# The FFN of a hybrid diffusion step: chunks of three and six token blocks, the six in scaled fp16 pairs

## The chip, the cores and the metric

The kernel runs on one core of a Trainium2 chip. The metric is the device time of one execution in microseconds (us). The engines are called as in the profile: PE (TensorE, matmuls), PEld (its weight loads), DVE (VectorE), ACT (ScalarE), POOL (GpSimd) and SP (SyncE, which issues most DMAs). A chance of "faster" or "slower" means by more than 0.3%.

## What is computed

One layer over 128 context tokens and 1024 latent tokens, D_MODEL = 1024. Attention and an mLSTM read one input projection and share one output projection; then comes a SwiGLU FFN with D_FF = 2816. All tokens use the same weights. The part that the change touches:

```python
def swiglu(h, w_gu, w_down):
    g, u = jnp.split(h @ w_gu, 2, axis=-1)
    return (jax.nn.silu(g) * u) @ w_down

# in trunk_layer, behind attention and mLSTM
    mix = jnp.concatenate([attn_o, hm], axis=-1) @ w_out
    x = x + g1 * mix
    h2 = rmsnorm(x, norm2_w) * (1 + sc2) + sh2
    x = x + g2 * swiglu(h2, w_gu, w_down)
# the result is rmsnorm(x, final_norm_w)
```

Inputs and results are fp32. `w_gu` is 1024 x 5632 (gate, then up), `w_down` is 2816 x 1024.

## The kernel before

The 1152 tokens are nine blocks of 128 (block 0 is the context). Three blocks make a chunk, so there are three chunks: c = 0, 1, 2. A precise product is made of three matmuls: both operands are split into a high and a low half, and high x high, high x low and low x high are added up in PSUM. In the input projection the halves are scaled fp16 (`Scaled`, `linear_tok`, `head_project`). In the output projection and the FFN they are fp32r (a 4-byte type that PE reads in one pass).

**FFN.** D_FF is 22 tiles of 128 columns. `gate_up` makes, for each tile and a whole chunk (384 tokens), gate and up: `products` runs 8 x 3 matmuls of 384 columns for each (L1271 to L1273). The tanh form of silu times up gives `tn` (L1298 to L1300), split into `hl`. `down` takes a group of four or five tiles (`GROUPS`, `LAST`) and adds their product with `w_down` to the residual `x1` (`three_blocks`, matmuls of 512 columns, L1090 to L1092; `add_gated`, L1079 and L1080). Every piece of weights is loaded and split for every chunk anew by `load_piece`: a DMA of 512 KB on SP's queue into `raw` (two buffers), ACT's copy to the high half (L152), the subtraction for the low half, two in three on POOL and one on DVE (L135 through `sub`). So `w_gu` and `w_down` are read three times.

**Around it.** `prefill` adds the mLSTM half of the output projection to `x1` of all blocks; blocks 6 to 8 go through x1_d in DRAM by way of the three `t2` buffers, which the loads of `hm` use too. `attention(c)` works head by head: score matmuls (L1000) into the only score buffer `S`, a maximum on DVE (L1002), exp on ACT (L1003), an fp16 pair of the probabilities (L1006, L1007), transposes by DMA, and for two heads together the values (L1024, L1025). `attn_out` adds the attention half of the output projection, `norm2` makes the FFN's input. `finish` and `down_last` make the final norm and write out.

**Order.** `weave(main, side, n_main, n_side)` runs a main generator and takes steps of a side one at a fixed rate. Chunk 0's FFN has attention of chunk 1 woven in (17 of 22 tiles), chunk 1's FFN that of chunk 2, chunk 2's FFN stands alone. The first part of attention of chunk 1 runs before, beside `prefill` and `attn_out(0)`. A planner (`schedule_with_timeline_sim`) then orders each engine's instructions by the program's order, by `hot` priorities and by its own model of time. After that each engine's queue runs in order, and so does SP's queue of DMAs. PSUM has four banks for `mm`, one for `po` and three for `S`.

The loop around the chunks, and the last one's end:

```python
            weave(main, chain(previous(c, cur), att), 18 * sum(nf for _, nf in GROUPS[:NG]) - 24, 50)
            emit(att)
            emit(attn_out(c + 1, nxt, oT, out_gates()))
            emit(groups(c, cur, GROUPS[NG:-1]))
            ...
            weave(chain(down(c, cur, f0, nf, 0), down(c, cur, f0, nf, 1)), n2, 6 * nf, 8)
```

## Time and profile before

| | us |
|---|---|
| runs (three) | 1620.82, 1625.18, 1626.45 |
| median | 1625.18 |
| span of the profiled execution (no other time of it is given) | 1626.0 |
| PE clock, mean share granted | 0.972 |
| attention of chunk 0 and prefill | about 460 to 640 |
| FFN of chunk 0 with attention of chunk 1 | about 640 to 1000 |
| FFN of chunk 1 with attention of chunk 2 | about 1000 to 1300 |
| FFN of chunk 2 | about 1300 to 1613 |

A row of busy time by stage gives the stretch, its length, then busy us and number of instructions of each engine, the granted share of PE's clock, the DMA engines' mean busy share and their GB/s. A row of single instructions in order of time gives start, length, engine, line, operation, output and inputs; one "x6" at its end stands for six in a row. A row of a group gives busy time, mean ns of one, and the engine's idle time ahead with what ended it. The bar of a matmul is its whole way through the array, so bars overlap: the distance of starts is the pace. Some matmul records can be missing.

### The profile page before, as it was taken

Reading aid. Unit: us, or ns where it says so; the run is one execution under the profiler, and the core shown is the slowest. Engines: PE = TensorE matmul, PEld = TensorE weight load, DVE = VectorE, ACT = ScalarE, POOL = GpSimd, SP = SyncE. Lnnn points to the kernel's source line nnn. Section 1 sums busy time; section 2 is a strip of 40 time slices with the busy share of each in tenths; the row PEclk is TensorE's granted clock in tenths of the full one; section 3 lists DMA queues with packets and bytes.
Section 4 is the critical chain, followed back from the end, with each engine's and each line's share of the span. In section 5 each row is a group of like instructions: output and inputs, shape, how many; then the busy total and the mean of one; then the engine's idle time right before and its main releaser. Section 6 shows DMA issues by size and latency. Waiting matters only on the chain. (4 is left out here: it accounts for less than half of the span.)

```text
span 1626.0 us, 23528 instructions
## 1 busy us (share of the span) xinstructions
PE 1517.4 (93%) x8688; PEld 1258.8 (77%) x8688; DVE 970.8 (60%) x2059; ACT 732.5 (45%) x1251; POOL 606.5 (37%) x387
## 2 busy tenths in 40 slices
PE   5899899899879768999999999999999999999996
PEld 2745566575557557998989899898898989899995
DVE  3843364958987665467672646777674474432445
ACT  3744252434544554545643344565562453333332
POOL 0411020404344514443435354444344444545443
PEclk8999999999999878999999999999999999999998
DMA  9355352201156855767873546777684445545441
GB/s 357 94 165 130 101 147 58 84 21 46 41 198 147 195 107 112 168 168 174 187 184 112 149 141 219 187 184 173 156 183 128 134 142 170 152 126 149 130 142 66
DMA packets 386313, 232.73 MB, mean 143 GB/s; under 512 B 169910, under 2 KB 346502, under 8 KB 386198
## 3 DMA queue, kind: packets, MB, share of 16 engines
q1 hardware_dynamic: 384342, 228.04, 52.7%
q10 hardware_dynamic: 1856, 3.19, 0.6%
q8 instruction: 68, 1.11, 0.3%
q14 instruction: 47, 0.39, 0.1%
HBM read 181.16 MB, written 11.69 MB: 119 GB/s over the span
## 5 line engine op out<-in xcount | busy, mean ns | idle before, releaser
L135 POOL TENSOR_TENSOR wlo<-raw,whi 128x1024 fp32r<-128x1024 f32 x146 | 357.8, 2454 | 445.7 <-ACT whi L152 407.9
L152 ACT CAST whi<-raw 128x1024 fp32r<-128x1024 f32 x219 | 224.4, 1025 | 375.9 <-DMA raw<-in_w_gu_dram 137.8
L1272 PE MATMUL mm<-aTl,whi 128*128 128x384 f32 (+2 forms) x1088 | 364.7, 335 | 0.7 <-POOL aTl L135 0.7
L1273 PE MATMUL mm<-aTh,wlo 128*128 128x384 f32 (+2 forms) x1088 | 364.4, 335 | 0.0
L1271 PE MATMUL mm<-aTh,whi 128*128 128x384 f32 (+2 forms) x1088 | 363.4, 336 | 0.7 <-DVE tn L1299 0.7
L1272 PEld LDWEIGHTS mm<-aTl,whi 128*128 128x128 f32 x1088 | 205.9, 189 | 1.7 <-POOL aTl L135 0.9
L1271 PEld LDWEIGHTS mm<-aTh,whi 128*128 128x128 f32 x1088 | 205.4, 189 | 2.0 <-DVE tn L1299 1.3
L1273 PEld LDWEIGHTS mm<-aTh,wlo 128*128 128x128 f32 x1088 | 205.8, 189 | 0.1
L135 DVE TENSOR_TENSOR wlo<-raw,whi 128x1024 fp32r<-128x1024 f32 (+1 forms) x73 | 88.1, 1206 | 142.2 <-ACT whi L152 141.7
L1090 PE MATMUL mm<-whi,hl 128*128 128x512 f32 x372 | 145.8, 397 | 1.5 <-ACT hl L1303 1.4
L1091 PE MATMUL mm<-wlo,hl 128*128 128x512 f32 x372 | 146.9, 397 | 0.0
L1092 PE MATMUL mm<-whi,hl 128*128 128x512 f32 x372 | 144.3, 396 | 0.7 <-POOL hl L135 0.7
L1007 DVE SCALAR_TENSOR_TENSOR pl<-pr,st,ph 128x1152 f16<-128x1152 f32 (+1 forms) x72 | 107.8, 1498 | 39.4 <-ACT ph L1006 39.4
L488 PE MATMUL wi<-ipair,hT 128*128 128x384 f16 (+2 forms) x392 | 128.2, 327 | 2.8 <-ACT ipair L216 2.8
L489 PE MATMUL wi<-ipair,hT 128*128 128x384 f16 (+2 forms) x392 | 128.1, 327 | 0.0
L490 PE MATMUL wi<-ipair,hT 128*128 128x384 f16 (+2 forms) x392 | 127.1, 326 | 0.0
L135 POOL TENSOR_TENSOR hl<-tn,hl 128x384 fp32r<-128x384 f32 x66 | 84.2, 1276 | 105.0 <-ACT hl L1303 105.0
L1003 ACT ACTIVATE pr<-S,st 128x1152 f32<-128x1152 f32 (+1 forms) x72 | 81.1, 1127 | 89.1 <-DVE st L1002 86.1
L1299 DVE SCALAR_TENSOR_TENSOR tn<-tn,mm 128x384 f32<-128x384 f32 (+2 forms) x68 | 36.7, 540 | 137.9 <-PE mm L1273 97.5
L1080 DVE TENSOR_TENSOR x<-x,t 128x512 f32<-128x512 f32 x102 | 116.5, 1163 | 0.8
L1000 PE MATMUL S<-kst,qT 128*128 128x384 f32 (+1 forms) x400 | 88.3, 355 | 19.6 <-ACT pr L1003 19.2
L1002 DVE TENSOR_REDUCE st<-S 128x1 f32<-128x1152 f32 (+1 forms) x72 | 88.9, 1234 | 18.3 <-PE S L1000 17.8
(353 smaller groups left out, 2684.6 us busy)
## 6 DMA issues: line engine op xcount, KB each, us to landing
raw<-in_w_gu_dram SPq DMA_DIRECT2D x132, 512.0 KB
raw<-in_w_down_dram SPq DMA_DIRECT2D x60, 512.0 KB
a<-in_w_ada_dram SPq DMA_DIRECT2D x32, 512.0 KB
gl<-g_d SPq DMA_DIRECT2D x36, 256.0 KB
aw<-in_w_ada_dram SPq DMA_DIRECT2D x16, 512.0 KB
iraw<-in_w_in_dram SPq DMA_DIRECT2D x32, 256.0 KB
raw<-in_w_out_dram SPq DMA_DIRECT2D x15, 512.0 KB
x<-in_x_sample_dram SPq DMA_DIRECT2D x13, 512.0 KB
```

What stands on the lines that cost most here:

```text
L135: (dve if eng == "dve" else pool).tensor_tensor(out=out, in0=full, in1=hi, op=ALU.subtract)
L152: nc.scalar.copy(hi[:, :n], raw[:, :n])
L488: mm(ps[:, :n], ah, wh[:, k % 2, c0 : c0 + n], start=(k == 0), stop=False)
L489: mm(ps[:, :n], ah, wl[:, k % 2, c0 : c0 + n], start=False, stop=False)
L490: mm(ps[:, :n], al, wh[:, k % 2, c0 : c0 + n], start=False, stop=(k == KD - 1))
L1080: eng.tensor_tensor(out=x1[:, cs], in0=x1[:, cs], in1=t, op=ALU.add)
L1090: mm(ps, ah, wh[:, k % 2, :], start=(k == 0), stop=False)
L1091: mm(ps, ah, wl[:, k % 2, :], start=False, stop=False)
L1092: mm(ps, al, wh[:, k % 2, :], start=False, stop=(k == nk - 1))
L1271: mm(ps, wh[:, k, :], th[:, k, :], start=(k == 0), stop=False)
L1272: mm(ps, wh[:, k, :], tl[:, k, :], start=False, stop=False)
L1273: mm(ps, wl[:, k, :], th[:, k, :], start=False, stop=(k == KD - 1))
```

## The change

Chunk 0 keeps its FFN in fp32r. Chunks 1 and 2 run theirs together, six blocks on one reading of the weights, in scaled fp16 pairs.

- Both attentions now run beside chunk 0's FFN: the rest of chunk 1's beside groups 0 and 1, chunk 2's beside groups 2 and 3 together with `norm2(1)`; `norm2(2)` beside the gates of group 4.
- `bound_h2` derives a power of two from the bounds of scale and shift; `norm2` of c > 0 uses scaled copies and writes fp16 pairs.
- `Piece` loads a tile's gate and up (1 MB), measures the sum of squares on ACT, sums it over partitions with a matmul of ones, makes a power of two in eight DVE operations, and converts (ACT the high, DVE the low half): loaded three tiles ahead, measured two ahead, converted one ahead. The first is done within the last `down` of chunk 0.
- `split_down` loads `w_down` tile by tile (512 KB), scales and splits it by partition, and writes the fp16 pair to DRAM (`wd_d`); `down6` reads these four times in quarters, two for each half of the blocks.
- `gate_up6` keeps `tn` of a whole group in fp32; `rescale` finds the group's scale and writes `hl`. Groups are of 10, 8 and 4 tiles (`SIX`). PSUM becomes eight banks.
- `prefill` sends blocks 3 to 8 through x1_d. `down`'s adds for chunk 0 go to POOL.

The diff, cut:

```diff
-LAST = [(0, 5), (5, 5), (10, 4), (14, 4), (18, 4)]
+SIX = [(0, 10), (10, 8), (18, 4)]
+SLOTS = 30
...
+    wd_d = [drp.tile([P, 2, 2, 2, 512], F16, name=f"wd_d{j}") for j in range(NF // 2)]
...
+    def bound_h2():
+        m = gp.tile([P, 4], F32, name="hb2")
+        dve.tensor_reduce(out=m[:, 0:1], in_=scale2, axis=AX.XY, op=ALU.max, apply_absolute_value=True)
+        dve.tensor_reduce(out=m[:, 1:2], in_=shift2, axis=AX.XY, op=ALU.max, apply_absolute_value=True)
...
+        yield from power_scale(gp, one1, m[:, 2:3], h2s)
...
-                    if c < 2:
-                        add_gated(x1s[c][i], ps, g, n, pool)
+                    if c == 0:
+                        add_gated(x1[i], ps, g, n, pool)
                     else:
                         xt = t2()
                         dma(xt, xrow(b)[:, cs])
                         t = t2()
                         dve.tensor_tensor(out=t, in0=ps, in1=g, op=ALU.mult)
                         pool.tensor_tensor(out=xt, in0=xt, in1=t, op=ALU.add)
-                        dma(x1_d[i][:, cs], xt)
+                        dma(x1_d[b - CB][:, cs], xt)
...
+    def split_down():
+        def load(f):
+            t = hp.tile([P, 3, 1024], F32, name=nm("wdt"), tag=f"b{2 + f % 2}")
+            dma(t[:, 0], w_down[f * P : (f + 1) * P, :])
+            return t
+        ahead = [load(0)]
+        for f in range(NF):
+            t = ahead.pop(0)
+            if f + 1 < NF:
+                ahead.append(load(f + 1))
+            yield
+            raw, v = t[:, 0], wds[:, f, :]
+            act(t[:, 2].bitcast(BF16)[:, 0:1024], raw, AF.Abs, accum_out=v[:, 0:1])
+            powers(v, P)
+            yield
...
+            act(o[:, :, 0], raw, AF.Copy, scale=v[:, 2:3])
+            dve.scalar_tensor_tensor(out=o[:, :, 1], in0=raw, scalar=v[:, 2:3], in1=o[:, :, 0], op0=ALU.mult, op1=ALU.subtract)
+            dma(wd_d[f // 2][:, :, f % 2], o)
+            yield
...
+        def measure(self):
+            v = self.v = fp.tile([P, 8], F32, name=nm("fv"), tag="fv", bufs=5)
+            for j, raw in enumerate(self.raw):
+                jk = ft.tile([P, D], BF16, name=nm("jk"), tag="t2", bufs=3)
+                act(jk, raw, AF.Square, accum_out=v[:, j : j + 1])
+        def scales(self):
+            v = self.v
+            ps = bank()
+            mm(ps[:, 0:2], ones, v[:, 0:2], start=True, stop=True)
...
+        def convert(self):
...
+                act(t[:, 0], raw, AF.Copy, scale=sc)
+                dve.scalar_tensor_tensor(out=t[:, 1], in0=raw, scalar=sc, in1=t[:, 0], op0=ALU.mult, op1=ALU.subtract)
...
+    weave(main, att, 18 * 8 - 24, 42)
+    emit(att)
+    one = {"x1": new_x1(1, "b6")}
+    emit(attn_out(1, one, oT, out_gates()))
...
+    weave(groups(0, cur, GROUPS[2:4]), chain(*[norm2(1, one, i) for i in range(CB)], att), 18 * 9, 48)
+    emit(att)
+    two = {"x1": new_x1(2, "b0")}
+    emit(attn_out(2, two, oT, out_gates()))
...
+    weave(gate_up(cur, f0, nf), n2, 12 * nf, 7)
+    emit(n2)
+    first = Piece(0, lambda: wp.tile([P, 1024], F32, name=nm("braw"), tag="raw", bufs=2))
+    emit(down(0, cur, f0, nf, 0))
+    for i, _ in enumerate(down(0, cur, f0, nf, 1)):
+        if i == 0:
+            first.load()
+        elif i == 1:
+            first.measure()
+        elif i == 3:
+            first.scales()
+        elif i == 4:
+            first.convert()
...
+    one["x1"] = new_x1(1, "b1")
...
+    pieces[1].load()
+    pieces[1].measure()
+    pieces[2].load()
...
+    emit(finish(0, cur))
...
+    wd_steps = split_down()
+    for _ in range(4):
+        next(wd_steps)
...
+                    products(ps[:, 0:CT], wh, wl, th, tl)
+                    step = 2 * half + j
+                    if step == 0:
+                        if f + 1 < NF:
...
+                            pieces[f + 1].convert()
+                        if f + 3 < NF:
+                            pieces[f + 3].load()
+                        p.fold()
+                        next(wd_steps, None)
+                    elif step == 1 and f + 2 < NF:
+                        pieces[f + 2].measure()
...
+                    elif step == 3:
+                        if f + 2 < NF:
+                            pieces[f + 2].scales()
+                        next(wd_steps, None)
...
+                act(tn, pg[:, 0:CT], AF.Tanh, scale=p.v[:, 6:7])
+                dve.scalar_tensor_tensor(out=tn, in0=tn, scalar=1.0, in1=pu[:, 0:CT], op0=ALU.add, op1=ALU.mult)
+                dve.scalar_tensor_tensor(out=tn, in0=tn, scalar=p.v[:, 7:8], in1=pg[:, 0:CT], op0=ALU.mult, op1=ALU.mult)
+                jk = ft.tile([P, D], BF16, name=nm("jk"), tag="t2", bufs=3)
+                act(jk[:, 0:CT], tn, AF.Abs, accum_out=g["st"][:, 2 * i + half : 2 * i + half + 1])
...
+        for tn in g["a"]:
+            hl = bp.tile([P, 2, CT], F16, name=nm("hl"), tag="hl", bufs=SLOTS)
+            act(hl[:, 0], tn, AF.Copy, scale=m[:, 1:2])
+            dve.scalar_tensor_tensor(out=hl[:, 1], in0=tn, scalar=m[:, 1:2], in1=hl[:, 0], op0=ALU.mult, op1=ALU.subtract)
...
+    def down6(g):
+        for half in range(2):
+            for n in range(2):
+                banks = [bank() for _ in range(CB)]
+                for j in range(0, g["nf"], 2):
+                    w = down_piece(g, j, n)
+                    for i, ps in enumerate(banks):
+                        b = half * CB + i
+                        down_products(ps, g, j, b, w)
+                        if j + 2 == g["nf"]:
+                            add_gated(x6[b], ps, g6[n], n, inv=g["inv"])
+                        yield
```

`groups6` runs a group's `down6` inside the next group's gates, and the last group's down runs block by block with the final norm, as `down_last` did.

More of the change, by code (lines that the diff above doesn't have):

```diff
@@ L908, in hybrid_step @@
     cc, ss = tables(kw)
-    kwork = k_work(qp, cc, ss, kw)
+    kwork = chain(k_work(qp, cc, ss, kw), bound_h2())
     scan = head_mlstm(2, sts[2])
-    weave(head_project(3, sts[3]), beside((scan, 1.15), (kwork, 0.5)), 56, 56)
+    weave(head_project(3, sts[3]), beside((scan, 1.15), (kwork, 0.55)), 56, 56)
     emit(scan)
@@ L1421, in previous @@
             yield
[L1423 to L1451 removed]
+            o = t[:, 1].bitcast(F16).rearrange("p (n h x) -> p n h x", n=2, h=2)
@@ new lines, in hybrid_step @@
+    main = groups(0, cur, GROUPS[:2])
+    for _ in range(4):
+        next(main)
+    weave(main, att, 18 * 8 - 24, 42)
+    emit(att)
+    one = {"x1": new_x1(1, "b6")}
+    emit(attn_out(1, one, oT, out_gates()))
+    oT = []
+    att = attention(2, oT, set())
+    weave(groups(0, cur, GROUPS[2:4]), chain(*[norm2(1, one, i) for i in range(CB)], att), 18 * 9, 48)
+    emit(att)
+    two = {"x1": new_x1(2, "b0")}
+    emit(attn_out(2, two, oT, out_gates()))
+    f0, nf = GROUPS[-1]
+    n2 = chain(*[norm2(2, two, i) for i in range(CB)])
@@ new lines, in hybrid_step @@
+    bp = ctx.enter_context(tc.tile_pool(name="bp", bufs=1, reuse_waits="tile"))
+    psum["mm"] = ctx.enter_context(tc.tile_pool(name="p8", bufs=8, space=PSUM, reuse_waits="tile"))
+    pieces = [first] + [Piece(f) for f in range(1, NF)]
+    pieces[1].load()
+    pieces[1].measure()
+    pieces[2].load()
+    h6 = [(t["h2"][:, 0], t["h2"][:, 1]) for t in (one, two)]
+    x6 = one["x1"] + two["x1"]
+    emit(finish(0, cur))
+    g6 = []
+    for n in range(2):
+        gl = ft.tile([P, 512], F32, name=nm("gl"), tag=("gl", "gx")[n], bufs=1)
+        dma(gl, g_d[1, 1:2, n * 512 : (n + 1) * 512].to_broadcast([P, 512]))
+        g6.append(gl)
@@ new lines, in groups6 @@
+    def groups6(grps):
+        held = None
+        for g in grps:
+            ups = gate_up6(g)
+            if held is not None:
+                r = rescale(held)
+                for _ in range(2):
+                    yield next(ups)
+                next(r)
+                for _ in range(2):
+                    yield next(ups)
+                emit(r)
+                for _ in range(2):
+                    yield next(ups)
+                if g["nf"] > 4:
+                    yield from down6(held)
+                    yield from ups
+                else:
+                    yield from ups
+                    d = down6(held)
+                    for _ in range(6):
+                        yield next(d)
+                    r = rescale(g)
+                    next(r)
+                    for _ in range(6):
+                        yield next(d)
+                    emit(r)
+                    yield from d
+            else:
+                yield from ups
+            held = g
```

255 lines of the change are left out of this document (153 added, 102 removed).

## The prediction

> **What bounds the kernel now.** I read the page's engine totals first, then busy time by stage, then single matmuls in order of time.
>
> ```profile
> span 1626.0 us, 23528 instructions
> PE 1517.4 (93%) x8688; PEld 1258.8 (77%) x8688; DVE 970.8 (60%) x2059; ACT 732.5 (45%) x1251; POOL 606.5 (37%) x387
> ...
> 460.00:640.00 180.00, 141.79 (x731) 114.43 (x731) 122.97 (x233) 90.72 (x137) 70.03 (x41) 0.89 0.64 150
> 640.00:1000.00 360.00, 355.50 (x1991) 326.38 (x1990) 217.36 (x327) 173.51 (x232) 152.51 (x73) 0.99 0.63 158
> 1000.00:1240.00 240.00, 236.09 (x1345) 215.69 (x1344) 156.20 (x215) 128.99 (x169) 99.75 (x47) 1.00 0.73 180
> 1240.00:1600.00 360.00, 358.17 (x1879) 331.77 (x1878) 165.95 (x229) 126.88 (x167) 172.80 (x86) 1.00 0.47 141
> 1600.00:1626.00 26.00, 13.20 (x57) 10.36 (x55) 16.99 (x54) 6.39 (x15) 3.85 (x3) 0.80 0.17 61
> ```
>
> The rows by stage give, behind the length, the busy us of PE, weight loads, DVE, ACT and POOL, then granted clock, DMA share and GB/s. From 640 us on (the FFN of all three chunks, with attention of chunks 1 and 2 woven in) PE is idle 4.5 + 3.9 + 1.8 = 10.2 us in 960, at a clock of 0.99 to 1.00. So PE sets the time there, and only two things can move it: how fast PE goes through its list, or idle time that is put in. Busy bars of matmuls overlap, so the pace is read from their starts:
>
> ```profile
> 1440.13 0.34 PE L1272 MATMUL mm<-aTl,whi 128*128 128x384 f32 x1
> ...
> 1441.86 0.34 PE L1273 MATMUL mm<-aTh,wlo 128*128 128x384 f32 x1
> 1442.04 0.39 PE L1090 MATMUL mm<-whi,hl 128*128 128x512 f32 x1
> ...
> 1445.99 0.39 PE L1092 MATMUL mm<-whi,hl 128*128 128x512 f32 x1
> 100.59 0.33 PE L488 MATMUL wi<-ipair,hT 128*128 128x384 f16 x1
> ...
> 102.86 0.33 PE L490 MATMUL wi<-ipair,hT 128*128 128x384 f16 x1
> 424.78 0.38 PE L488 MATMUL mm<-ipair,hT 128*128 128x512 f16 x1
> ...
> 425.86 0.38 PE L490 MATMUL mm<-ipair,hT 128*128 128x512 f16 x1
> 1072.01 0.28 PE L1025 MATMUL po<-plT,vs 128*128 128x256 f16 x1
> ...
> 1072.78 0.27 PE L1024 MATMUL po<-phT,vs 128*128 128x256 f16 x1
> ```
>
> Between the first two rows lie 10 steps: 1.73/10 = 0.173 us for 384 columns of fp32r. The next two: 17 steps, 3.95/17 = 0.232 us for 512. In fp16, which the input projection already uses, 14 steps of 2.27 give 0.162 for 384, and 5 steps of 1.08 give 0.216 for 512. Fp32r costs some 7% more per column.
>
> **The change, part by part.** *Pace.* One tile of 128 FFN columns takes, for three token blocks, 2 x 8 x 3 = 48 matmuls of 384 columns (gate, up) and 3 x 2 x 3 = 18 of 512 (down). The number of matmuls stays; for six of nine blocks they become fp16. Gate and up: 22 x 48 x 2 = 2112 x (0.173 - 0.162) = 23.0 us. Down: 22 x 18 x 2 = 792 x (0.2324 - 0.216) = 13.0 us. Together **-36.0 us**, all on PE's path. This is the whole source of gain: the weights are read and split less often, but POOL (37%), ACT and DMA were not in PE's way.
>
> The Trainium skill, page "TensorE: Matmul & The Clock Gate", section "Back-to-back issue gap", speaks against it: its formula for the warm gap is columns / 2.4 + 2.5 ns, whatever the data type, that is 162.5 and 215.8 ns. The fp16 rows agree with it (0.162, 0.216); the fp32r rows (0.173, 0.232) don't. By that formula the type gains nothing, this term is zero and the sum would be 36 us higher.
>
> *Matmuls added.* Each gate/up tile gets one fp32 matmul of two columns with a matrix of ones (`scales`), which sums the squares over partitions. Three groups and the bound of h2 add a transpose and a two-column matmul each.
>
> ```profile
> L324 PEld LDWEIGHTS wi<-strip_sel,part 128*128 128x128 f32 x32 | 3.7, 191 | 3.2 <-ACT part L356 3.2
> L324 PE MATMUL wi<-strip_sel,part 128*128 128x2 f32 x32 | 3.9, 252 | 1.4 <-ACT part L356 1.4
> ```
>
> Nearest is a two-column fp32 matmul: its weight load of 0.19 us hides under the matmul before (0), or lies bare with the matmul behind it (0.44). I take the load alone: 22 x 0.19 = **+4.2** (0 to 9.7). The four others, two small matmuls of 0.25 each with a little between: 4 x 0.55 = **+2.2**. Each `scales` also waits for ACT's measure, and behind it in PE's queue stand the next products; the measure is issued two runs of 24 matmuls, 7.8 us, ahead of it, which covers some 2.5 us of work on ACT.
>
> *Chunk 0 carries both attentions.* So far attention of chunk 1 is woven into 17 tiles of chunk 0 and that of chunk 2 into 17 of chunk 1. Now the rest of the first lies in 8 tiles and the second in 9, beside norm2 of chunk 1.
>
> ```profile
> 640.00:860.00 220.00, 26.40 (x120) 21.57 (x120) 0.98 0.73 169
> 1000.00:1220.00 220.00, 29.74 (x144) 24.99 (x144) 1.00 0.76 186
> ...
> 1060.00:1120.00 60.00, 60.00 (x349) 54.42 (x348) 46.55 (x61) 34.40 (x46) 25.33 (x11) 1.00 0.73 173
> ...
> L1002 DVE TENSOR_REDUCE st<-S 128x1 f32<-128x1152 f32 x64 | 86.6, 1353 | 17.6 <-PE S L1000 17.3
> L1007 DVE SCALAR_TENSOR_TENSOR pl<-pr,st,ph 128x1152 f16<-128x1152 f32 x64 | 103.5, 1617 | 39.2 <-ACT ph L1006 39.2
> L1029 DVE SCALAR_TENSOR_TENSOR oT<-po,vsc,ol 64x128 f32<-64x128 f32 x72 | 24.6, 342 | 16.9 <-ACT ol L1027 15.6
> L1299 DVE SCALAR_TENSOR_TENSOR tn<-tn,mm 128x384 f32<-128x384 f32 x64 | 35.3, 552 | 136.1 <-PE mm L1273 97.5 <-ACT tn L1298 38.0 <-issue 0.3
> L135 DVE TENSOR_TENSOR wlo<-raw,whi 128x1024 fp32r<-128x1024 f32 x67 | 83.9, 1252 | 118.0 <-ACT whi L152 117.6 <-issue 0.4
> L1079 DVE TENSOR_TENSOR t<-mm,gl 128x512 f32<-128x512 f32 x106 | 70.7, 684 | 39.5 <-PE mm L1092 17.6 <-DMA gl<-g_d 10.4 <-PE mm L1358 6.7
> L1245 DVE TENSOR_SCALAR fl<-mm,scale,shift 128x128 f32<-128x128 f32 x66 | 22.5, 403 | 1.8 <-PE mm L114 1.7
> ```
>
> The first two rows count the score matmuls (L1000), six to a head: 24 heads in 220 us, 9.2 us each. In the second new weave 9 tiles take 9 x (48 x 0.173 + 18 x 0.232) = 112 us and 24 heads about 24 x (6 x 0.173 + 9 x 0.11) = 49 (nine matmuls of 256 columns a head): 161/24 = 6.7 us a head. The first weave, 8 tiles and 120/6 = 20 heads, is about as dense: 141/20 = 7.0. DVE per head: 1.35 + 1.62 + 0.34 and about 0.4 of small operations (an estimate) = 3.7. A tile of the FFN: two of 0.55, one lower half in three of its pieces (1.25), six multiplies of 0.68 to four or five tiles (0.9) = 3.3, since the adds now go to POOL; 0.375 tiles a head = 1.2. Norm2 of chunk 1: six halves of 4 x 0.40 and a subtraction of some 0.7 = 14 us, 0.6 a head. That is 5.5 of 6.7, 82%. At 1060 to 1120 DVE was busy 78% and PE 60.00 of 60. So it fits, with little room: I take **+4** (lower bound -5, half the 10.2 of idle time gone; upper bound in the rivals). ACT is lower: its 128.99 of 240 us in the 1000:1240 row, times 9.2/6.7, is 74%.
>
> *Prefill.* Blocks 3 to 5 now go through `t2` buffers and x1_d as 6 to 8 did: six more round trips on SP's queue, each some 512 KB, at a DMA share of 0.64 (row 460:640). All nine hm blocks share the three `t2` buffers, so DVE can wait for a store, and attention's reductions stand behind it. **+1** (0 to 8). `bound_h2` adds some 14 small DVE operations, under 3 us, hidden beside the head projection.
>
> *Entering the six blocks.* The first fp16 tile is loaded, measured, scaled and converted during the last down-projection of chunk 0.
>
> ```profile
> 1352.81 6.72 DMA raw<-in_w_gu_dram
> L199 ACT ACTIVATE jk<-iraw 128x1024 bf16<-128x1024 f32 x20 | 21.2, 1058 | 7.6 <-DMA iraw<-in_w_in_dram 7.3 <-issue 0.3
> L216 ACT ACTIVATE ipair<-iraw,isc 128x1024 f16<-128x1024 f32 x10 | 11.5, 1152 | 1.9 <-PE wi L490 1.8
> L217 DVE SCALAR_TENSOR_TENSOR ipair<-iraw,isc,ipair 128x1024 f16<-128x1024 f32 x10 | 16.0, 1612 | 8.6 <-ACT ipair L216 8.6
> ```
>
> A 512 KB load took 6.7 us to land in the chain of waits; two beside each other I put at 8. Then the second measure (1.06 + 0.19), the sum (0.25), eight DVE operations (1.2), the first high half (1.15): 12 us, with hand-overs 13. Cover: the load stands behind two of 15 units of three matmuls, 13 x 3 x 0.232 = 9 us. Uncovered **+4** (0 to 20). The sum's wait stands in PE's queue ahead of the last down matmuls, and DVE's adds for chunk 0 wait for those.
>
> *Inside the six.* A tile's gate/up lasts 96 x 0.162 = 15.6 us. ACT does two converts (2.3), two measures (2.5), w_down's measure and high half (2.4), two tanh and two absolute sums of 384 columns (an estimate from 1.06 for 1024: about 2.3): 9.5. DVE does two lower halves (3.2), that of w_down (1.6), four multiplies of about 0.55 and some 13 small ones: 9. Both fit, at about 60%. DMA moves 1 MB of w_gu, 0.5 in and 0.5 out of w_down: 2 MB in 15.6 us, 128 GB/s, where 180 was seen. `rescale` has 20 copies each on ACT and DVE, about 12 us, behind 16 us of other products. I take **+2** (0 to 10).
>
> *The end.* A block of the last down now takes PE 24 x 0.216 = 5.2 us; its DVE work is 5.5 to 6.7.
>
> ```profile
> 1612.80 0.40 PE L1358 MATMUL mm<-whi,hl 128*128 128x512 f32 x1
> ...
> 1610.95 1.81 DVE L1080 TENSOR_TENSOR x<-x,t 128x512 f32<-128x512 f32 x1
> ...
> 1616.66 0.68 DVE L1080 TENSOR_TENSOR x<-x,t 128x512 f32<-128x512 f32 x1
> ...
> 1621.35 0.16 DVE L131 SCALAR_TENSOR_TENSOR ry<-rt,ry 128x1 f32<-128x1 f32 x1
> 1621.54 0.75 DVE L1369 SCALAR_TENSOR_TENSOR x<-x,ry,fw 128x512 f32<-128x512 f32 x1
> ```
>
> (Two multiplies of 0.68, as L1079 above, two adds of 0.68 to 1.81, twelve of about 0.16 for the root, one of 0.75.) DVE already starts its last operation 8.7 us after the last matmul. Six blocks instead of three let it fall further behind: **+3** (0 to 6).
>
> *Sum:* -36.0 + 4.2 + 2.2 + 1 + 4 + 4 + 2 + 3 = -15.6, so a span of 1610.4 from 1626.0. The runs' median, 1625.18, is within 1 us of that span, so the forecast is 1610.
>
> **Rivals.**
> 1. *All the new work is hidden.* Only the added matmuls remain: 1626 - 36 + 6.4 = 1596. For it: the old changes of stage cost PE next to nothing (10.2 us in 960). Against: entering the six has an uncovered chain in the program's order.
> 2. *The entry is bound by transfers.* Ahead of the first w_down tile stand in program order 1 MB, 1.5 of x1, 2 more of weights, about 1 of gates and gains: 6 MB, at 180 GB/s 33 us from the first load. If ACT's order puts its measure in front of the second tile's convert, due about 29 us in, that comes at some 36 to 42 us: 7 to 13 us more. Time 1617 to 1630, say 1623: no change that can be measured.
> 3. *Slower: attention binds PE in chunk 0.* In 460:640 PE idled 38.2 us while 130 score matmuls, 21.7 heads, ran (first row): 1.8 us a head, and the score buffer heads the list of waits there (second row):
>
> ```profile
> 460.00:640.00 180.00, 30.67 (x130) 25.00 (x130) 0.89 0.64 150
> ...
> PE S L1000 <- ACT pr L1003: 15.4, 6, 3.7
> ```
>
> If the 24 heads of the second weave ran so, that is 43 us in place of the 4: 1610 - 4 + 43 = 1649; with the first weave at a third of it as well it is beyond 1655, and two thirds as bad in the second alone is 1635. It decides once DVE's 5.5 us and its waits pass 6.7 a head, since one score buffer is shared. Against it stand 78% of DVE with no idle PE.
> 4. *The change doesn't speed PE up:* the 7% belongs to the FFN's stage and not to fp32r, so 1610 + 36 = 1646. The page's formula would have it so. Against: the 256-column fp16 matmuls of attention, in that stage, go at 0.77/7 = 0.110, the fp16 pace (0.162 x 256/384 = 0.108).
>
> **Chances.** About 0.3%, 5 us, is what a measurement can tell from no change: faster is below 1620, slower above 1630. Forecast (1600 to 1620) 0.48; rival 1 0.15; rival 2 with other small losses (1620 to 1630) 0.17; rival 3 0.16; rival 4 0.04. Faster 0.63, same 0.17, slower 0.20. The range 1592 to 1634 takes in all of the forecast and rival 2, most of rival 1 and the mild end of rival 3; about 0.2 is left out. It spans -34 to +8 in the sum, most of the unknown bounds.
>
> **What would show it.** Starts of 384-column matmuls 0.162 apart and of 512-column ones 0.216 in the six's stage; PE idle there below 5 us; a gap of some 4 us before the first six-block tile; in chunk 0, PE idle below 15 us and DVE near 80% in the second weave; DVE's end 10 to 15 us after the last matmul. It is wrong if fp16 goes at 0.173 there, if PE waits on scores or on `scales` by tens of us, or if DVE or ACT come near 90% within the six.

## The result and the profile after

The changed kernel takes 1690.14 us (median of four runs, 1684.76 to 1694.7), the kernel before in the same session 1623.95 (1620.82 to 1626.45): a ratio of 1.0412, 95% interval 1.0381 to 1.0443. It is 66 us slower, where 15 less were forecast. The profiled execution has a span of 1683.0 against 1626.0, so it shows 57 of the 66; the execution profiled after is the fastest of the four.

The head of the page after, to be laid beside the two lines of before:

```profile
span 1683.0 us, 23816 instructions
PE 1514.7 (90%) x8744; PEld 1051.5 (62%) x8744; DVE 983.9 (58%) x2389; ACT 771.3 (46%) x1410; POOL 377.5 (22%) x285
```

PE has as much busy time as before in a longer span. No engine has become full: DVE went from 60% to 58%, ACT from 45% to 46%. So something waits, and the rows by stage (columns as in the prediction's) say where:

```profile
460.00:640.00 180.00, 137.25 (x658) 107.56 (x656) 123.93 (x228) 88.05 (x135) 64.71 (x39) 0.87 0.65 157
640.00:860.00 220.00, 195.71 (x1140) 173.92 (x1139) 141.39 (x223) 117.74 (x159) 93.55 (x48) 0.95 0.66 161
860.00:980.00 120.00, 120.00 (x693) 110.10 (x692) 81.83 (x115) 68.03 (x92) 57.18 (x31) 1.00 0.74 169
980.00:1100.00 120.00, 90.08 (x430) 75.60 (x429) 72.20 (x113) 56.75 (x75) 29.25 (x15) 0.82 0.62 149
1100.00:1160.00 60.00, 51.88 (x261) 41.81 (x260) 30.95 (x82) 33.96 (x51) 20.14 (x13) 0.91 0.68 218
1160.00:1660.00 500.00, 500.00 (x2856) 279.60 (x2854) 231.82 (x562) 195.49 (x358) 3.81 (x3) 1.00 0.38 122
```

The six blocks (1160 to 1660) run PE for 500.00 of 500 us at full clock. All of the loss lies ahead of them: PE is idle 24.3 us in 640 to 860, nothing in 860 to 980, 29.9 in 980 to 1100 and 8.1 in 1100 to 1160, 62 us in a stretch (640 to 1160) where the kernel before had 7.8. The clock granted in the three stages with idle time is 0.82 to 0.95, where before it was 0.98 to 1.00. The list of PE's waits in 640 to 1160 (total, times, longest, us) names no single cause:

```profile
PE S L1023 <- ACT pr L1026: 16.6, 5, 6.7
PE mm L116 <- ACT y L1262: 13.7, 2, 9.3
PE po L1048 <- DMA plT<-pl: 8.8, 8, 1.9
PE mm L1300 <- ACT wpair L1467: 7.5, 1, 7.5
PE mm L1148 <- ACT mx L1220: 6.6, 2, 3.3
```

From the top: scores that wait for the score buffer, norm2's transposes, values that wait for transposes by DMA, the first tile of the six, and attn_out.

To split the 57 us, each matmul is counted at the median distance of starts of its kind in the same trace. That gives PE's list; what is left of a stage is idle time (gaps between bars) and slow time (starts further apart than the median). The stages are cut at the first FFN matmul of 384 columns (its rows stand with e13), the first of the six and the end of the last.

| us | before | after |
|---|---|---|
| until the FFN starts | 646.1 | 658.2 |
| PE's list from there to the last matmul | 948.4 | 917.8 |
| idle and slow, up to the six (before: all the rest) | 18.8 | 60.2 + 28.3 = 88.5 |
| idle and slow, in the six | | 5.1 |
| from the last matmul to the end | 12.8 | 13.4 |
| span | 1626.1 | 1683.0 |

PE's list became 30.6 us shorter, as forecast (29.6). The FFN starts 12 us late, and up to the six PE loses some 70 us that it did not lose before. Those two are what the experiments are about.

### The profile page after: what moved, and what is told of

The parts are those of the page before. It is cut to its first block, busy times and chain, and to the rows that moved or that the text cites. A ratio compares the mean times of both kernels' runs of the same rounds, so it can differ in the third digit from the quotient of the medians.

```text
span 1683.0 us, 23816 instructions
## 1 busy us (share of the span) xinstructions
PE 1514.7 (90%) x8744; PEld 1051.5 (62%) x8744; DVE 983.9 (58%) x2389; ACT 771.3 (46%) x1410; POOL 377.5 (22%) x285
## 5 line engine op out<-in xcount | busy, mean ns | idle before, releaser
L1300 PE MATMUL mm<-h,wpair 128*128 128x384 f16 x704 | 230.6, 328 | 7.5 <-ACT wpair L1467 7.5
L1302 PE MATMUL mm<-h,wpair 128*128 128x384 f16 x704 | 230.5, 327 | 0.7 <-DVE wpair L1468 0.7
L1301 PE MATMUL mm<-h,wpair 128*128 128x384 f16 x704 | 230.6, 328 | 0.0
L137 POOL TENSOR_TENSOR wlo<-raw,whi 128x1024 fp32r<-128x1024 f32 (+1 forms) x55 | 136.3, 2480 | 227.5 <-ACT whi L154 223.6
L1030 DVE SCALAR_TENSOR_TENSOR pl<-pr,st,ph 128x1152 f16<-128x1152 f32 (+1 forms) x72 | 110.7, 1538 | 47.6 <-ACT ph L1029 47.3
L1301 PE MATMUL mm<-aTl,whi 128*128 128x384 f32 (+2 forms) x384 | 128.2, 334 | 0.7 <-POOL aTl L137 0.7
L1300 PE MATMUL mm<-aTh,whi 128*128 128x384 f32 (+2 forms) x384 | 128.1, 335 | 0.1
L1302 PE MATMUL mm<-aTh,wlo 128*128 128x384 f32 (+2 forms) x384 | 127.4, 332 | 0.0
L1664 POOL TENSOR_TENSOR x<-x,fw 128x512 f32<-128x512 f32 x6 | 7.6, 1267 | 521.4 <-ACT jk L1661 521.4
L1023 PE MATMUL S<-kst,qT 128*128 128x384 f32 (+1 forms) x400 | 93.9, 372 | 33.7 <-ACT pr L1026 33.7
L154 ACT CAST whi<-raw 128x1024 fp32r<-128x1024 f32 (+1 forms) x83 | 85.0, 1025 | 76.3 <-PE mm L1301 23.8
L1025 DVE TENSOR_REDUCE st<-S 128x1 f32<-128x1152 f32 (+1 forms) x72 | 88.8, 1234 | 30.4 <-PE S L1023 29.9
L1300 PEld LDWEIGHTS <-wpair 128*128 128x128 f16 x704 | 70.7, 100 | 52.6 <-ACT wpair L1467 7.9
L1023 PEld LDWEIGHTS S<-kst,qT 128*128 128x128 f32 x400 | 77.0, 210 | 40.6 <-ACT pr L1026 38.0
L1596 PE MATMUL mm<-wd,hl 128*128 128x512 f16 x264 | 100.1, 379 | 0.0
L1597 PE MATMUL mm<-wd,hl 128*128 128x512 f16 x264 | 100.1, 379 | 0.0
L1598 PE MATMUL mm<-wd,hl 128*128 128x512 f16 x264 | 100.1, 379 | 0.0
L1302 PEld LDWEIGHTS <-wpair 128*128 128x128 f16 x704 | 69.1, 98 | 47.3 <-DVE wpair L1468 1.3
```

The source lines that it names most:

```text
L137: (dve if eng == "dve" else pool).tensor_tensor(out=out, in0=full, in1=hi, op=ALU.subtract)
L1023: mm(S[:, n, 0:w], qT[:, h, :], kst[kv][:, t, c0 + n * w : c0 + (n + 1) * w], start=(t == 0), stop=(t == 1))
L1030: dve.scalar_tensor_tensor(out=plv, in0=prv, scalar=st[:, 3:4], in1=phv, op0=ALU.mult, op1=ALU.subtract)
L1300: mm(ps, wh[:, k, :], th[:, k, :], start=(k == 0), stop=False)
L1301: mm(ps, wh[:, k, :], tl[:, k, :], start=False, stop=False)
L1302: mm(ps, wl[:, k, :], th[:, k, :], start=False, stop=(k == KD - 1))
```

## The experiments

**Theory 1**: the chain of a head is too slow, since the lower half of its probabilities (1.6 us, L1030 after) stands in DVE's queue ahead of the next head's maximum. **Theory 2**: the order of PE's queue. Heads need cover, that is, FFN matmuls that keep PE busy while a head's chain runs on DVE, ACT and DMA. Each head gets some 6 us of FFN, whatever rate the program asks for; the 17 tiles are used up before the heads are, and the heads that are left come bare, with no FFN matmul between them. All runs are compared with the kernel before in the same session; ratios below are against it.

**e1 and e2: the lower half behind the next maximum**, in the kernel after and before.

```diff
-                    dve.scalar_tensor_tensor(out=plv, in0=prv, scalar=st[:, 3:4], in1=phv, op0=ALU.mult, op1=ALU.subtract)
+                    def low(after=None, plv=plv, prv=prv, phv=phv, st=st, o=plT[:, h % 2, 0:nk, :]):
+                        s = st[:, 3:4]
+                        if after is not None:
+                            s = st[:, 4:5]
+                            dve.scalar_tensor_tensor(out=s, in0=after, scalar=0.0, in1=st[:, 3:4], op0=ALU.mult, op1=ALU.add)
+                        dve.scalar_tensor_tensor(out=plv, in0=prv, scalar=s, in1=phv, op0=ALU.mult, op1=ALU.subtract)
+                        nc.sync.dma_start_transpose(o, plv.rearrange("p a b -> p (a b)"))
+                    lows.append(low)
...
+                        lows.pop()(st[:, 0:1])
```

The next head calls it behind its exp, with its own maximum (times zero) in the scalar, so that the order is forced.

> The changed kernel, with DVE's order in attention forced: the lower half of a head's probabilities stands behind the next head's maximum (one operation of about 0.15 us a head added). Theory 1 (one head is a chain of about 7 us, because the next maximum waits in DVE's queue behind a lower half that waits for ACT; chunk 0 has too little FFN to cover 44 such heads): a head falls to about 5 us where attention runs alone, PE's idle time at the end of both weaves (about 50 us in the changed kernel) falls by half or more, 1640 to 1660 us. Theory 2 (the chain is not the point; FFN is used up too early by the order, and the output projection and norm2 behind attention stand bare): within 10 us of the changed kernel, 1680 to 1700.

> The same forced order in the kernel before. Theory 1: from 640 us on nothing moves, since 17 tiles cover a chunk's 24 heads at 9 us each; at most the stage from 460 to 640 us gains, 1605 to 1625 us. Theory 2: 1620 to 1630, no change.

Measured: 1698.41 us, ratio 1.0451 (1.0434 to 1.0468), and 1629.55, 1.0026 (1.0009 to 1.0044). Nothing is gained in either. Theory 1, as put, falls.

**e3: attention at a higher rate** in both weaves.

```diff
-    weave(main, att, 18 * 8 - 24, 42)
+    weave(main, att, 18 * 8 - 24, 60)
-    weave(groups(0, cur, GROUPS[2:4]), chain(...), 18 * 9, 48)
+    weave(groups(0, cur, GROUPS[2:4]), chain(...), 18 * 9, 72)
```

> The changed kernel with attention taken faster in both weaves (60 for 42 and 72 for 48 steps), so that FFN is kept for the end. Theory 1: the chain sets the pace of heads whatever the program's order, 1680 to 1695 us. Theory 2: FFN is left to cover the end of attention, the output projection and norm2, 1650 to 1670 us.

Measured: 1677.29, 1.0324 (1.0307 to 1.0341), 13 us back. Where FFN covers them, heads still come 8.0 us apart in the first weave and 7.5 in the second (7.8 and 7.9 in the kernel after), at a rate that asks for much less. The rate in the program is not what sets the spacing. Theory 2 had expected 1650 to 1670.

**e4: the first tile of the six earlier**: loaded ahead of the first half of the last down, into another buffer, with the measure one step sooner and sum and conversion two.

```diff
+    early = hp.tile([P, 3, 1024], F32, name=nm("braw"), tag="b2")
...
+    first.load()
     emit(down(0, cur, f0, nf, 0))
...
```

> The changed kernel with the first fp16 tile loaded before the last two down products, not within the last one, and measured, scaled and converted two steps earlier. If the 8 us of idle PE at the entry to the six blocks is the load's latency, they go: 1680 to 1685 us. If they come from ACT's or DVE's queue there, the time stays at about 1690.

Measured: 1696.33, 1.0447 (1.0423 to 1.0471), no gain. The wait moved from the first product (7.5) to the sum (6.2), and 14 us of small gaps came up inside the six, which had had 0.7. What PE finds waiting there is not the first tile alone.

**e5, e6 and e7: an order tied by hand.** In e5 every FFN step is queued on PE behind the last score matmul that the program has issued (an order without a wait). In e6 norm2(1) stands behind attention(2) as well. In e7 the rate of e6 is higher (52 and 60).

```diff
+                with tc.issue_after(last_s[0].ins):
+                    units = next(it, end)
...
-    ..., chain(*[norm2(1, one, i) for i in range(CB)], att), 18 * 9, 48)
+    ..., chain(att, *[norm2(1, one, i) for i in range(CB)]), 18 * 9, 48)
```

> The changed kernel with the order on PE held in both weaves: an FFN matmul is queued behind the last score matmul that precedes it in the program, so a head gets the 4.7 us of FFN that the weave gives it, not the 6 us that the planner puts in. Theory 2 (the planner's pace, 8 us a head, uses the FFN up after some 33 of 44 heads; the chain itself would allow less): heads come every 6.5 to 7 us, few are left bare at the end of the weaves, 1635 to 1665 us. Theory 3 (the queues of DVE and ACT can't do a head in less than 8 us beside FFN): heads stay at 8 us, PE now idles within the weaves, 1685 to 1710.

> As e5_paced, and norm2 of chunk 1 behind attention of chunk 2 in the side, so that PE's queue doesn't stand at its transposes (9.3 us of one wait in the changed kernel) when FFN could go on. Theory 2: 5 to 15 us under e5_paced. If FFN behind the transposes can't go on for other reasons (weights, banks): the same as e5_paced.

> As e6_paced_norm2_late, with attention taken faster (52 for 42 and 60 for 48 steps), which leaves a head 3.8 us of FFN. If the chain of scores, maximum and exp (4.2 us without hand-overs) is the floor, a head of 3.8 + 2 us is about at it and FFN is left to cover the output projections: 10 to 20 us under e6. If a head can't go below 6.5 us in practice, PE idles within the weave instead: the same as e6 or slower.

Measured: 1684.24, 1.0375 (1.0345 to 1.0404); 1668.78, 1.0283 (1.0252 to 1.0314); 1674.91, 1.0309 (1.0271 to 1.0347). From the first to the last start of the second weave, heads now come 6.8, 6.4 and 6.4 us apart, and the last starts at 1025, 986 and 994 us instead of 1041. So a tie in the order brings heads nearly as fast as the program asks (6.7; 5.8 in e7), which the rate alone did not, and theory 3 falls. But the time doesn't follow: e5 lies 19 us above the range expected of it, e6 is 15 under e5, e7 is no faster than e6. The best order gives 21 of 66 us back. Inside both weaves of e6, and in the list of PE's waits from 695 to 986:

```profile
695.00:793.00 98.00, 86.39 (x493) 76.89 (x491) 67.37 (x95) 58.30 (x75) 34.93 (x19) 0.95 0.78 166
837.00:986.00 149.00, 135.29 (x792) 123.66 (x791) 105.70 (x150) 95.39 (x126) 61.43 (x30) 0.97 0.84 190
```

```profile
PE S L1041 <- ACT pr L1044: 12.9, 5, 4.3
```

PE idles 25.3 us although FFN stands between nearly all heads, half of it for the score buffer; DVE is busy 71% in the second weave. In e7 the two weaves idle 44 us. At some 6.5 us a head, what PE waits for is the chain of the heads themselves.

**e8 and e9: eight heads less**, after and before. Attention of block 8 is left out, its attention output is zero.

```diff
+            if b == 8:
+                late.pop()()
+                yield
+                oT.append(new_oT())
+                dve.memset(oT[i], 0.0)
+                done.add(i)
+                return
```

> The changed kernel, but attention for the last token block (block 8, eight heads of the 64 that go over all keys) is left out: its attention output is set to zero. Everything else stays. The work left out is 8 x (6 x 0.173 + 9 x 0.11) = 16 us of PE. Theory 2 (the order gives every head some 6 us of FFN, so that the cover of 17 tiles is used up at about 985 us and the last eleven heads come bare, 5 to 9 us apart): the eight heads that go are among the bare ones, so the last head comes at about 990 instead of 1041 and the time falls by 40 to 55 us, to 1635 to 1650; PE idle between 980 and 1040 falls from some 27 us to below 8. Rival (the loss of 66 us is spread over the whole stage and does not hang on where the cover ends): the time falls by PE's work alone, 14 to 22 us, to 1668 to 1676.

> The kernel before with the same heads left out (block 8's attention output is zero). There every head has cover, the heads of chunk 2 end before the 17 tiles do. Both theories: the time falls by PE's work alone, about 16 us (14 to 20), to some 1606 to 1610. The difference of this fall to that of the changed kernel is what the heads cost beyond PE's work when they are bare: theory 2 says 25 to 40 us, the rival 0 to 5.

Measured: 1635.03, 1.0077 (1.0055 to 1.0099), and 1606.26, 0.9902 (0.9879 to 0.9925). The same heads cost the changed kernel 1690.1 - 1635.0 = 55 us and the kernel before 1622.1 - 1606.3 = 16, which is PE's work for them and nothing else. So 39 us of the loss are eight heads without cover. Counted as in the table, the two traces of the changed kernel show 30 of the 39: 21.4 us of idle and 8.9 of slow time. The stretch in which they ran, of the kernel after and of e8:

```profile
980.00:1040.00 60.00, 37.78 (x173) 28.78 (x172) 37.72 (x52) 31.19 (x38) 12.17 (x7) 0.75 0.78 172
```

```profile
980.00:1040.00 60.00, 51.02 (x248) 42.54 (x247) 35.59 (x58) 25.19 (x34) 20.48 (x12) 0.91 0.62 162
```

PE's idle time falls from 22.2 to 9.0 us there, and the clock rises from 0.75 to 0.91. The 9.0 that stay (expected: below 8) are attn_out, which in e8 stands in the same place.

Why the cover ends early is seen in the second weave of the kernel after, in the counts of one line (behind the length, PE's busy us and number): scores (L1023), one of the three gate and up lines (L1302), and one of the three down lines (L1116). The last two rows are scores and gates behind it.

```profile
871.00:989.00 118.00, 18.86 (x90) 1.00 0.76 171
871.00:989.00 118.00, 33.51 (x100) 1.00 0.76 171
871.00:989.00 118.00, 21.12 (x54) 1.00 0.76 171
989.00:1045.00 56.00, 15.37 (x54) 0.72 0.78 170
989.00:1045.00 56.00, 0.00 (x0) 0.72 0.78 170
```

90/6 = 15 heads in 118 us: 7.9 us a head. Beside them stand 3 x 100 x 0.173 + 3 x 54 x 0.232 = 89.5 us of FFN, 6.0 us a head. The program asked for 4.7 (112 us for 24 heads). Then FFN is used up, and nine heads follow bare. The kernel before, in its second weave, shows nearly the same spacing with the same lines (L1000, L1271, L1090):

```profile
1015.00:1200.00 185.00, 26.83 (x131) 22.36 (x129) 1.00 0.75 177
1015.00:1195.00 180.00, 54.56 (x161) 1.00 0.74 176
1015.00:1195.00 180.00, 28.20 (x72) 1.00 0.74 176
```

131/6 heads in 185 us are 8.5 us a head, with 3 x 161 x 0.173 + 3 x 72 x 0.232 = 133.7 us in 180, 6.3 us of FFN to each. So both kernels lay the heads out nearly alike. Before, two chunks gave 34 tiles to cover 44 heads; now 17 tiles have to, some 212 us, of which some 36 run where no head starts (680 to 696, 809 to 871). The last four heads of the first weave (from 789 to 808) and the last nine of the second come bare, and each time attn_out behind them.

**e10: one part of the change alone.** The kernel before, with only gate and up of chunk 2 in scaled fp16 pairs; attention stays where it was.

```diff
-            yield from gate_up(a, f0, nf)
+            yield from (gate_up if c < 2 else gate_up16)(a, f0, nf)
...
+                    if j == 0 and k == 3 and f + 1 < NF:
+                        pieces[f + 1].scales()
+                if j == 0:
+                    if f + 1 < NF:
+                        pieces[f + 1].convert()
+                    if f + 3 < NF:
+                        pieces[f + 3].load()
+                    if f + 2 < NF:
+                        pieces[f + 2].measure()
+                    p.fold()
```

`gate_up16` is `gate_up` with the change's `Piece` in it; the down-projections take `hl` and `w_down` in fp32r as before.

> The kernel before, with one part of the change alone: only gate and up of chunk 2, whose FFN stands alone, use scaled fp16 pairs (measured, scaled and converted there, the first tile during the last group of chunk 1). The order of attention, the down-projections and the split of w_down stay as they were. 22 x 48 = 1056 matmuls at 0.162 instead of 0.173: -11.6 us; 22 matmuls of the sums at 0.05 to 0.44, by what the changed kernel's six showed about 0.1 to 0.2: +2 to +4. Theory 2 (the conversion to fp16 is worth what was worked out, and the loss lies in the order of chunk 0 alone): faster by 5 to 9 us, a ratio of 0.994 to 0.997. Rival (measuring and scaling beside the products costs PE as much as fp16 gives): 1.000 to 1.005; PE would then be idle by more than 5 us between 1310 and 1600, or wait on the sums.

Measured: 1616.6 us (1615.32 to 1617.64) against 1622.07, ratio 0.9963 (0.9949 to 0.9978). It is the only version here that does all the work and is faster than the kernel before, by 0.4%. PE in its chunk 2, two products ten steps apart:

```profile
1399.83 0.33 PE L1487 MATMUL mm<-h,wpair 128*128 128x384 f16 x1
...
1401.46 0.33 PE L1488 MATMUL mm<-h,wpair 128*128 128x384 f16 x1
```

And its sums (count, shortest, median and longest in ns, first and last start):

```profile
L1450 PE MATMUL mm<-fv,ones x42: 167/210/251, 1328.5 to 1570.6; 128*128 128x2 f32 x42
```

1.63/10 = 0.163 us for a product, and 0.21 for a sum's bar, two to a tile. PE's list from the FFN's start to the last matmul is 7.8 us shorter (expected: 11.6 less 2 to 4), and that stretch 5.1 (962.0 for 967.1), since 5 us of idle time came up in it. The rival (conversion costs PE as much as it gives) falls, as long as conversion has an FFN to itself. One thing stays open: in this profile the FFN also starts earlier, at 639.3 for 646.1, which the change was not meant to do, so a part of the 5.5 us by the medians may come from there.

**e11 and e12: more cover**, on the kernel after and on e6. The gates of group 4 join the second weave; norm2(2) moves to the first half of group 4's down.

```diff
-    weave(groups(0, cur, GROUPS[2:4]), chain(...), 18 * 9, 48)
+    weave(chain(groups(0, cur, GROUPS[2:4]), gate_up(cur, f0, nf)), chain(...), 18 * 9 + 12 * nf, 66)
...
-    weave(gate_up(cur, f0, nf), n2, 12 * nf, 7)
-    emit(n2)
-    emit(down(0, cur, f0, nf, 0))
+    weave(down(0, cur, f0, nf, 0), n2, 3 * nf, 7)
+    emit(n2)
```

> The changed kernel, with the gates of group 4 (5 tiles, 240 matmuls of 0.173 = 41.5 us of PE) put behind groups 2 and 3 in the second weave, so that attention of chunk 2 has them as cover too; norm2(2) moves from beside them to beside the first half of group 4's down. No work is left out. Theory 2: the eleven heads that came bare from 985 to 1041 now have FFN between them, PE's idle time of 29.9 us in 980 to 1100 and the slow clock behind it go for the most part; attn_out(2) still stands bare, and norm2(2) has 10 us of cover instead of 41. The time falls by 20 to 35 us, to 1655 to 1670. Rival (the heads are late for a reason of their own, by DVE or the score buffer, and the idle time follows them): below 8 us less, 1682 or more.

> The same on top of the paced order with norm2(1) behind attention (1668.8 us, last head at 986 us). Theory 2: there only the end of the second weave and attn_out(2) were still bare (4.9 + 8.2 us of idle at 1040 and 1100, and 7.1 at 840), so more cover is worth 5 to 12 us, to 1657 to 1664; still slower than the kernel before by 2%, since the entry to the six, the bare attn_out and the stalls within the six (9 us) remain. Rival: 0.

Measured: 1677.33, 1.0332 (1.0291 to 1.0372), and 1673.86, 1.0326 (1.0267 to 1.0384). e11 gives 13 us back and not 20 to 35; e12 is no faster than e6, where 5 to 12 less were expected (their intervals overlap). The rows of e11, and its longest wait of PE in 1040 to 1160:

```profile
980.00:1040.00 60.00, 58.14 (x340) 53.77 (x339) 42.09 (x51) 35.69 (x46) 30.00 (x17) 1.00 0.92 211
1040.00:1160.00 120.00, 89.06 (x436) 66.80 (x435) 84.36 (x200) 72.27 (x111) 24.35 (x13) 0.84 0.80 246
```

```profile
PE mm L116 <- ACT y L1262: 15.0, 1, 15.0
```

In the heads' stretch the idle time is gone (22.2 to 1.9 us). In 1040 to 1160, where the kernel after had 15.8, it has become 30.9: now norm2(2) has lost its cover and waits 15 us. In e12 the same wait is 18.7. So theory 2 is right about the heads, but my expectations took the cover for something that could be added; it was taken from the next step.

**e13 and e14: chunk 1's x1 kept on the chip**, on the kernel after and on e6: prefill adds blocks 3 to 5 straight to it, as before.

```diff
-                    if c == 0:
-                        add_gated(x1[i], ps, g, n, pool)
+                    if c < 2:
+                        add_gated(x1s[c][i], ps, g, n, pool)
```

> The changed kernel, but prefill adds blocks 3 to 5 straight to a resident x1 of chunk 1, as the kernel before does, instead of through t2 buffers and x1_d. In the changed kernel the first FFN matmul of 384 columns starts at 658.2 us, before at 646.1: 12 us are lost ahead of the FFN, for which the prediction had 1. Theory A (the six more round trips, by the three t2 buffers that they share with the loads of hm): the FFN starts at 645 to 650, the time falls by 8 to 13 us, to 1677 to 1682. Theory B (bound_h2, whose operations stand in front of prefill: its first 512-column matmul comes at 466.3 instead of 457.8): the FFN still starts at 655 to 660 and the time falls by less than 4 us. Against B speaks that with bound_h2 alone (gate and up of chunk 2 in fp16) the first 512-column matmul came at 465.3 too, and the FFN at 639.3.

> The same on top of the paced order with norm2(1) behind attention (1668.8 us, FFN from 657.6). Theory A: 8 to 13 us less, 1656 to 1661, still slower than the kernel before by some 2%. Theory B: 1665 or more. Both: what then is left over the kernel before is idle and slow time of PE in the stage of chunk 0, 40 to 55 us, against the 31 us that fp16 takes off the list of PE.

Measured: 1668.66, 1.0274 (1.0248 to 1.03), 21 us back, and 1646.81, 1.0128 (1.0093 to 1.0163), 22 less than e6. Both are more than the 8 to 13 expected. The first gate matmuls of the FFN (L1271 before, L1300 later; each row: durations in ns, first and last start), of the kernel before, after, and e13:

```profile
L1271 PE MATMUL mm<-aTh,whi x13: 220/276/420, 645.9 to 651.7; 128*128 128x128 f32 x12, 128*128 128x384 f32 x1
```

```profile
L1300 PE MATMUL mm<-aTh,whi x15: 220/274/393, 658.0 to 663.8; 128*128 128x128 f32 x11, 128*128 128x384 f32 x4
```

```profile
L1300 PE MATMUL mm<-aTh,whi x17: 221/274/391, 644.7 to 650.5; 128*128 128x128 f32 x14, 128*128 128x384 f32 x3
```

The FFN starts 13.3 us sooner, at the time of the kernel before. The wait behind it, in 460 to 660, of the kernels before, after and e13:

```profile
PE mm L114 <- DMA t<-hm_d: 1.7, 1, 1.7
```

```profile
PE mm L116 <- DMA t<-hm_d: 10.4, 2, 5.3
```

```profile
PE mm L116 <- DMA t<-hm_d: 4.9, 2, 3.3
```

The loads of hm come late when three more blocks pass through the same `t2` buffers and x1_d. So the round trips cost the 12 us, and bound_h2, which is in both, does not. Whether it is by the three buffers, as theory A has it, is not shown: SP's queue, which issues those loads in order, also stands at the stores of the round trips until POOL has made their data. Its waits there in 440 to 660, of the kernels before, after and e13:

```profile
SPq L1175 <- POOL t L1174: 4.6, 4, 2.2
```

```profile
SPq L1201 <- POOL t L1200: 12.9, 8, 4.0
```

```profile
SPq L1201 <- POOL t L1200: 6.7, 4, 3.8
```

Of the 21 us the profile shows 9 (span 1673.6 for 1683.0), so the size beyond 9 to 13 rests on the medians alone. Of e14's 17 us of span (1645.8 for 1662.8), 10 lie ahead of the FFN; the six are 14 shorter, since gaps of 10 us that e6 had there are gone, and chunk 0 is 6 longer. Why, no run tells.

## Why the prediction was wrong, step by step

- **Pace: right.** Starts in the six of the kernel after, ten steps of gate and up and two of down:

```profile
1299.74 0.33 PE L1302 MATMUL mm<-h,wpair 128*128 128x384 f16 x1
...
1301.37 0.33 PE L1300 MATMUL mm<-h,wpair 128*128 128x384 f16 x1
...
1668.72 0.38 PE L1596 MATMUL mm<-wd,hl 128*128 128x512 f16 x1
...
1669.15 0.38 PE L1598 MATMUL mm<-wd,hl 128*128 128x512 f16 x1
```

1.63/10 = 0.163 and 0.43/2 = 0.215. Rival 4 is out: in the same trace gates in fp32r keep a median of 0.173. The Trainium skill's formula ("TensorE: Matmul & The Clock Gate", section "Back-to-back issue gap") gives the fp16 numbers (162.5 and 215.8 ns). It names no data type; taken for every type it would have made this term zero, and the 0.173 disagrees.
- **Matmuls added: right.** The six's list is 517.2; products alone are 2112 x 0.162 + 792 x 0.216 = 513.2. The rest is 4.0 where 6.4 was put.
- **Inside the six: right in kind.** Idle and slow together 5.1, put at 2 above nothing.
- **The end:** 0.6 instead of 3.
- **Entering the six:** the wait on the first tile is 7.5 instead of 4, inside its bounds of 0 to 20. It was ACT's high half, at the end of the chain, as worked out; e4 shows that starting the chain sooner does not shorten the time.
- **Prefill: right mechanism, wrong size.** 12 us (13 by e13) instead of +1, above its bound of 8. Six round trips were counted, but as DMA share. They cost through hm's loads, for which PE waits; the paragraph had named the three shared buffers, but for DVE's wait.
- **"Chunk 0 carries both attentions": this step failed.** It was put at +4 and came to 62 (88.5, less 18.8 of before and 7.5 of the entry). Two things in it were wrong. First, it took the spacing of heads from the program's rate, 6.7 us a head. The kernel before had 8.5 from start to start (the 9.2 read from the row counts the time from 1000 to 1015, in which no head starts), and that spacing came along, as 7.9. So thirteen heads came bare. They are 18.4 us for the three distances from 789 to 808 and 52.0 for the eight from 989 to 1041; less 2.0 of PE's own work a head that makes 70.4 - 22 = 48 us, and what is left of the 62 fits the waits at attn_out and norm2 (6.6 and 13.7 us in PE's list). Second, it asked only whether DVE could keep up. It could: in 860 to 980 DVE is busy 81.83 of 120 us, 68% and not 82%, and in e6, with heads 6.4 us apart, 71%. But there PE still idles 25 us in the two weaves: the waits along a head's chain, which need no busy engine, had no price in the sum.
- **The rivals.** The time went beyond rival 3, at the place that rival 3 named, but not by its mechanism: DVE never became the bound, and the score buffer is 16.6 of the 62 idle us. Where heads come as close as the sum had them (e6, e7) the score buffer does head PE's list, with 14.3 and 18.7 us in 640 to 1160, and still without a full DVE. Its price per bare head was also too low (1.8 us idle, from a stage with prefill beside it; e8 and e9 show 39/8 = 4.9, with the slow time in it).

What stays open: the 42 us of idle and 19 of slow time that e14 still has in chunk 0. They are waits of several kinds, and no order tried here removed them. The largest sum, of PE's waits in 640 to 1180 of e14:

```profile
PE S L1041 <- ACT pr L1044: 14.9, 8, 3.0
```

That any order would make six blocks in fp16 pay was not shown.

## What to carry to other kernels

Work that hides under other work needs its cover counted at the spacing the trace shows, not at the one the program asks for: here 8.5 us a head stood in the kernel before, and halving the cover left thirteen heads and both attn_out bare. Where the order can be tied closer, the waits along the chain need a price too, even if no engine is full. When a gain of 36 us needs two stages merged, first try the part that needs no merging (e10, 5 us faster). And when idle time is taken out of one place, look in the next stage before calling it gained: e4, e11 and e12 moved it.

## What was not expected of the hardware

Idle time is paid for again, in part. Behind the last head of the kernel after, attn_out's matmuls of 512 columns (start and length in us):

```profile
1045.74 0.80 PE L1148 MATMUL mm<-whi,mx 128*128 128x512 f32 x1 [3.30 <-ACT mx L1220]
...
1046.77 0.63 PE L1148 MATMUL mm<-whi,mx 128*128 128x512 f32 x1
...
1050.61 0.63 PE L1148 MATMUL mm<-whi,mx 128*128 128x512 f32 x1
```

Nine steps in 3.84 us are 0.427 each, where 0.232 is the pace, and the clock granted in 1046 to 1051 was 0.50. It took some 5 us from the end of the wait to the full pace. Over chunk 0 this slow time is 28.3 us beside 60.2 of idle time, an addition of nearly half that the prediction did not have in any term. The Trainium skill ("TensorE: Matmul & The Clock Gate", section "What's actually happening") has the clock halved after an idle window of about 3.4 us and until a busy one has passed. The trace agrees with that length: every change of the clock in chunk 0 lies on a grid of 3.41 us (996.6, 1010.2, 1017.1, 1023.9, 1027.3 and on). But a single wait need not be that long, and the window need not be empty. Windows of the grid (behind the length, PE's busy us and number, then the clock):

```profile
1010.24:1013.65 3.41, 1.67 (x11) 1.00 0.00 0
1013.65:1017.06 3.41, 1.46 (x7) 1.00 0.78 150
1017.06:1020.48 3.42, 2.24 (x11) 0.50 0.96 199
1020.48:1023.89 3.41, 3.41 (x14) 0.50 1.19 209
1023.89:1027.30 3.41, 0.61 (x4) 1.00 1.02 340
```

Behind 1.67 us of busy bars the clock stays full, behind 1.46 it is halved, and behind 2.24 it is not yet given back. So the waits of 0.9 to 6.7 us between bare heads are enough to bring it about; with attn_out, norm2 and the entry to the six the clock falls eleven times between the FFN's start and the six.

In these rows the 7% of fp32r is not there at the half clock. Values in fp16, just ahead of that wait and at a clock of 0.50, have these starts:

```profile
1038.05 0.42 PE L1047 MATMUL po<-phT,vs 128*128 128x256 f16 x1
...
1040.61 0.42 PE L1047 MATMUL po<-phT,vs 128*128 128x256 f16 x1
```

Twelve steps in 2.56 us are 0.213 for 256 columns, 0.83 ns a column; the fp32r rows above are 0.427/512, 0.83 too.
